# Gated DeltaNet on one Trainium2 core: gates moved behind the first taps, solver blocks transposed on 128 rows, weight subtractions shared out anew

## The chip, the cores and the metric

The kernel runs on one core of one Trainium2 chip. The core has five engines with an instruction queue each: PE (TensorE, matmuls into PSUM), ACT (ScalarE), DVE (VectorE), POOL (GpSimd) and SP (SyncE, which issues the DMAs here). Each queue runs in its written order; an instruction waits until what it reads has been written and what it overwrites has been read. The metric is the device time of one execution in microseconds (us). Before the change it was 2079.87 us, the median of three runs (2078.89 to 2080.14).

## The reference

The program is a decoder trunk of two layers over 512 tokens of width 1024. Each layer is a feed-forward block, a mixer, and another feed-forward block. The mixer of layer 0 is a convolution module; that of layer 1, which the change touches, is a chunked gated DeltaNet with 8 heads of 128 and chunks of 64 tokens. Cut to what matters:

```python
proj = h @ w_in                                  # q, k, v, z, and per head a, b
qkv = silu(causal_dwconv(qkv, w_sconv))          # 4 taps
g = -exp(a_log) * softplus(a + dt_bias)          # the gates
beta = sigmoid(b)
g = cumsum(g)                                    # within a chunk
decay = exp(where(causal, g_i - g_j, -inf))
A = where(strict, (k * beta) @ k.T * decay, 0)   # 64 x 64 for each head and chunk
Tm = inverse of (I + A), by a unit triangular solve
u = Tm @ (v * beta)
w = Tm @ (k * beta * exp(g))
# then a scan over the 8 chunks with a 128 x 128 state for each head
```

## The kernel before

All data lie with features (or tokens) on the 128 rows (partitions) of SBUF. Each weight block of 128 x 1024 is split into a rounded part and a rest, so that a product is three matmul passes: `hi` copies the loaded block `raw` to `whi` on ACT (L1071), `lo` subtracts to get `wlo` (L1077), and `mm3` (L172 to L174) does the passes. The list `LOP` says for which tiles `lo` runs on POOL; for the others it runs on DVE. Before, these are 4, 5 and 17 to 24.

**The steps.** The projection of the DeltaNet runs in a hand-written order. Tile 0 holds a and b, tiles 1 to 8 are the heads of k, 9 to 16 of q, 17 to 24 of v. Tiles 0 to 2 come from the stage before; `step(p)` computes tile p for p = 3 to 24 with 24 matmuls of 128 x 512, three for each k from 0 to 7. Between these matmuls it writes the work on earlier tiles into the engines' queues: after k = 0 `mul` (first tap, ACT, L1097) of tile p-1 and `hi` of p+2; after k = 1 the other taps of p-1 (`tap`, DVE, L1100), and on PE `tr` of p-2 (four transposes through PE, L1121), for which `silu` of p-2 (ACT, L1114, for q L1111) must be done; after k = 2 `fin` of p-2 and `lo` of p+2; after k = 5 `silu` of p-1. From tile 18 on, the third tap is a multiply on ACT (L1104) and an addition on POOL (`ptap`, L1105). `fin` takes the squares of k and q on ACT (L1044, L1132); for v it multiplies by beta into `vb`, in one DVE instruction (L1127).

**The gates.** `tok_in`, `small_gates` and `gates_math` make g and beta of all heads and tokens: three exponentials on ACT (L976 to L979) and some 20 operations of 128 x 32 on DVE (L971 to L1001). `first_evac`, in step 3, writes them among the taps of tiles 1 and 2. `cumulate` (L1006), `decay` (L1013) for each head, `decay_mask` and `decay_exp` follow; the tables `DEC`, `DXA` and `DXB` name step and k for each.

**The solver.** All 64 matrices I + A (8 heads, 8 chunks; two chunks lie above each other on the 128 rows) are inverted by their 32 x 32 diagonal blocks, as one batch on DVE. `blk_in` transposes the blocks from `am` into `blk`, one quarter (32 rows) at a time (four instructions, L1167). `solve_a` and `solve_b` (L1171, L1176), 31 of each, do a substitution; `blk_out` transposes the result into `rm` (four, L1181), `low_out` into `lm` (two, L1185). `merge_a` and `merge_b`, in steps 23 and 24, join the blocks. These tasks stand in a queue, each with a weight; `inv_run` takes tasks up to a weight at four places of each step from 13 on (`IQ`: 2, 2, 3 and 3). A transpose weighs `IW` = 3, a solver operation 1. `blk`, `tmp`, `tb` and `lm` are quarters of the buffer `x`, which is spilled to DRAM meanwhile.

Of the kernel before, what the change touches and what calls it, by code (L numbers as in the profile page):

```python
# [11 lines left out]
ALU = mybir.AluOpType  # L12
# [3 lines left out]
P = 128  # L16
# [44 lines left out]
EH = [1,2,3,3,5,6]  # L61
FH = [3,4,5,6]
EN = {(0,1):2,(0,2):3,(1,0):3,(1,1):3,(1,2):3}
LOP = [4,5,17,18,19,20,21,22,23,24]
IW = 3
IQ = [2,2,3,3]
DEC = [(5,4),(5,6),(6,4),(6,6),(7,4),(7,6),(8,4),(8,6)]
DXA = [(6,7),(8,7)]
DXB = [(7,7),(9,7)]
KBK = [(11,2),(11,4),(11,6),(12,0),(12,2),(12,4),(12,6),(13,0)]  # L70
ZF = 1
RQ = (22,6)
# [34 lines left out]
def trunk_kernel(ctx: ExitStack, tc: tile.TileContext, x_in, c_in, vecs, consts, w_ada, w_st,  # L107
# [827 lines left out]
    def deltanet(layer, nxt):  # L935
        NU = HEADS * NG
        norm = Norm()
        with tc.tile_pool(name=nm("dn"), bufs=1) as dp, \
# [27 lines left out]
            def tok_in():  # L966
                act.copy(tok.rearrange("p c h -> p (c h)"), st["pt"][:, :NG * 16])

            def small_gates():
                xa = sm()  # L970
                dve.tensor_tensor(xa, tok[:, :, :HEADS],  # L971
                                  V("dt_bias", 0, HEADS).unsqueeze(1).to_broadcast([P, NG, HEADS]), ALU.add)
                nx = sm()
                dve.scalar_tensor_tensor(nx, xa, -1.0, xa, ALU.mult, ALU.max)
                ea = scratch("ea", (P, HEADS))
                act.activation(ea, V("a_log", 0, HEADS), AF.Exp)  # L976
                act.activation(beta.rearrange("p h c -> p c h"), tok[:, :, HEADS:], AF.Exp, scale=-1.0)
                ey = sm()
                act.activation(ey, nx, AF.Exp, scale=-1.0)  # L979
                st["g"] = xa, ey, ea  # L980
# [87 lines left out]
            def hi(p):  # L1068
                whi = wp.tile([P, KT, P], F32R, tag="whi", name=nm("whi"))
                wlo = wp.tile([P, KT, P], F32R, tag="wlo", name=nm("wlo"))  # L1070
                act.copy(whi, raws[p])  # L1071
                W[p] = whi, wlo
# [22 lines left out]
            def mul(p):  # L1095
                ct[p] = scratch("t", bufs=2)
                act.mul(ct[p], ps[p], taps_w(p, 0))  # L1097
# [25 lines left out]
            def fin(p):  # L1123
                g, m = kind(p)
                pt = kx.pop(p)
                if g == "v":
                    dve.tensor_tensor(vb[:, :, m, :], pt.rearrange("p (c e) -> p c e", e=P),  # L1127
                                      beta[:, m, :].unsqueeze(2).to_broadcast([P, NG, P]), ALU.mult)
                    return
                squares(pt, m, ssk if g == "k" else ssq)  # L1130
                if g == "k":
                    act.copy(kt[:, :, m, :], pt.rearrange("p (c d) -> p c d", d=P))  # L1132
# [28 lines left out]
                pool.memset(rm[CH:, :, :], 0.0)  # L1161
                pool.memset(rm[:CH, :, :], 0.0)

            def blk_in(q):
                rows = slice(q * 32, (q + 1) * 32)
                c0 = (q % 2) * 32
                dve.transpose(blk[rows], am[rows, :, c0:c0 + 32].rearrange("p u j -> p j u"))  # L1167

            def solve_a(j):
                n = 31 - j  # L1170
# [3 lines left out]
            def solve_b(j):  # L1174
                n = 31 - j
                dve.tensor_tensor(tb[:, j + 1:, :j + 1], tb[:, j + 1:, :j + 1], tmp[:, :n, :j + 1], ALU.subtract)  # L1176

            def blk_out(q):
                rows = slice(q * 32, (q + 1) * 32)
                c0 = (q % 2) * 32  # L1180
                dve.transpose(box["rm"][rows, :, c0:c0 + 32].rearrange("p u i -> p i u"), tb[rows])  # L1181

            def low_out(q):
                rows = slice(q * 32, (q + 1) * 32)
                dve.transpose(lm[rows].rearrange("p u l -> p l u"), tb[rows].rearrange("p i l -> p l i"))  # L1185

            def inv_tasks():
                for q in range(4):
                    inv_q.append((IW, lambda q=q: blk_in(q)))
                for j in range(31):  # L1190
                    inv_q.append((1, lambda j=j: solve_a(j)))
                    inv_q.append((1, lambda j=j: solve_b(j)))
                for q in (3, 1, 2, 0):
                    inv_q.append((IW, lambda q=q: blk_out(q)))
                for q in (0, 2):
                    inv_q.append((IW, lambda q=q: low_out(q)))

            def inv_run(n):
                while n > 0 and inv_q:
# [116 lines left out]
            def on(p, k, f):  # L1316
                ex.setdefault(p, {}).setdefault(k, []).append(f)

            def first_evac():
                mul(1)  # L1320
                tok_in()
                small_gates()
                mul(2)
                for d in (1, 2, 3):
                    tap(1, d)
                gates_math()
                for d in (1, 2, 3):
                    tap(2, d)
                for p in (4, 5):
                    hi(p)  # L1330
                    lo(p)
                inv_fill()
                silu(1)
                silu(2)

            on(3, -1, tok_tr)
            on(3, 0, first_evac)
            on(4, 0, lambda: tr(1))
            on(4, 3, lambda: tr(2))
            on(4, 3, lambda: fin(1))  # L1340
            on(4, 4, lambda: fin(2))
            on(4, 4, cumulate)
            for h in range(HEADS):
                p, k = DEC[h]
                on(p, k, lambda h=h: decay(h))
# [422 lines left out]
```

## Time and profile before

| what | time |
|---|---|
| median of three runs | 2079.87 us |
| the profiled execution | 2082.37 us |
| its span, first to last instruction | 2080.6 us |
| the DeltaNet's steps 3 to 24 in it | 1345.63 to 1536.09 us |

A row of a view by groups gives line, engine, operation, what is written from what, shapes, count, then busy us and mean ns of one, then the idle time of the engine ahead of it and what ended it. A row in order of time gives start and duration in us. A row of a stretch gives its length, then for each engine the busy us and the number of instructions, then the granted PE clock and the DMA share.

### The profile page before, as it was taken

Reading aid. Unit: us, or ns where it says so; the run is one execution under the profiler, and the core shown is the slowest. Engines: PE = TensorE matmul, PEld = TensorE weight load, DVE = VectorE, ACT = ScalarE, POOL = GpSimd, SP = SyncE. Lnnn points to the kernel's source line nnn. Section 1 sums busy time; section 2 is a strip of 40 time slices with the busy share of each in tenths; the row PEclk is TensorE's granted clock in tenths of the full one; section 3 lists DMA queues with packets and bytes.
Section 4 is the critical chain, followed back from the end, with each engine's and each line's share of the span. In section 5 each row is a group of like instructions: output and inputs, shape, how many; then the busy total and the mean of one; then the engine's idle time right before and its main releaser. Section 6 shows DMA issues by size and latency. Waiting matters only on the chain.

```text
span 2080.6 us, 26152 instructions
## 1 busy us (share of the span) xinstructions
PE 2009.1 (97%) x10330; PEld 1677.3 (81%) x10330; DVE 1201.0 (58%) x1824; ACT 767.6 (37%) x1316; POOL 213.4 (10%) x145
## 2 busy tenths in 40 slices
PE   6999999998899999999999999989899999999998
PEld 4888888877898888888888888877677798888887
DVE  6666666798865656536333333677955564333334
ACT  5422222474642222224222222465356643222222
POOL 0000000299100000000000000125410100000000
PEclk9999999999899999999999999999899999999999
DMA  7667767322236666532333333322121132333331
GB/s 269 233 220 238 230 228 234 112 75 90 60 110 207 201 197 205 165 92 81 103 99 96 98 100 91 102 71 72 61 62 32 42 121 91 102 94 98 96 98 61
DMA packets 78333, 262.06 MB, mean 126 GB/s; under 512 B 8321, under 2 KB 14081, under 8 KB 78082
## 3 DMA queue, kind: packets, MB, share of 16 engines
q1 hardware_dynamic: 77666, 259.87, 39.2%
q8 instruction: 81, 1.33, 0.3%
q10 hardware_dynamic: 544, 0.52, 0.1%
q14 instruction: 42, 0.34, 0.0%
HBM read 254.59 MB, written 5.77 MB: 125 GB/s over the span
## 4 chain that ended last, share of the span: by engine, by line
PE 85%; DVE 7%; POOL 3%; ACT 2%; issue 2%; DMA 0%; POOLq 0%; DVEq 0%; SPq 0%; ACTq 0%
PE mm L172 26%; PE mm L173 26%; PE mm L174 26%; POOL pacc L671 3%; DVE t L1100 1%; PE mm L1425 1%; DVE x L1176 1%; DVE x L1171 1%; PE mm L1447 1%; PE mm L1652 1%; PE mm L1653 1%; PE mm L1433 1%; PE mm L1656 1%; PE mm L1415 1%; PE aux L639 1%
## 5 line engine op out<-in xcount | busy, mean ns | idle before, releaser
L172 PE MATMUL mm<-hh,whi 128*128 128x512 f32 (+1 forms) x1968 | 744.9, 380 | 5.4 <-ACT hh L273 3.7
L173 PE MATMUL mm<-hl,whi 128*128 128x512 f32 (+1 forms) x1968 | 738.5, 376 | 1.6 <-DVE hl L277 1.3
L174 PE MATMUL mm<-hh,wlo 128*128 128x512 f32 (+1 forms) x1968 | 736.7, 375 | 1.9 <-DVE wlo L164 1.9
L164 DVE TENSOR_TENSOR wlo<-raw,whi 128x1024 fp32r<-128x1024 f32 (+1 forms) x291 | 356.1, 1225 | 306.7 <-ACT whi L163 301.9
L172 PEld LDWEIGHTS mm<-hh,whi 128*128 128x128 f32 x1968 | 372.5, 190 | 74.2 <-ACT hh L273 4.5
L174 PEld LDWEIGHTS mm<-hh,wlo 128*128 128x128 f32 x1968 | 373.3, 190 | 69.7 <-DVE wlo L164 2.9
L173 PEld LDWEIGHTS mm<-hl,whi 128*128 128x128 f32 x1968 | 373.6, 190 | 68.3 <-DVE hl L277 3.7
L163 ACT CAST whi<-raw 128x1024 fp32r<-128x1024 f32 (+1 forms) x291 | 297.2, 1023 | 285.4 <-PE mm L173 258.2
L172 PE MATMUL mm<-ahi,whi 128*128 128x512 f32 (+1 forms) x768 | 289.3, 377 | 0.0
L174 PE MATMUL mm<-ahi,wlo 128*128 128x512 f32 (+1 forms) x768 | 287.0, 374 | 0.0
L173 PE MATMUL mm<-alo,whi 128*128 128x512 f32 (+1 forms) x768 | 284.7, 371 | 0.0
L540 ACT CAST ahi<-t 128x512 fp32r<-128x512 f32 x88 | 54.7, 622 | 371.0 <-DVE t L536 371.0
L174 PEld LDWEIGHTS mm<-ahi,wlo 128*128 128x128 f32 x768 | 144.6, 188 | 28.2
L173 PEld LDWEIGHTS mm<-alo,whi 128*128 128x128 f32 x768 | 144.8, 188 | 27.0
L172 PEld LDWEIGHTS mm<-ahi,whi 128*128 128x128 f32 x768 | 145.0, 189 | 24.2
L425 DVE CUSTOM_DVE_ANT_0 ajunk<-araw,cs 128x1024 bf16<-128x1024 f32 x128 | 156.1, 1219 | 0.6
L532 ACT ACTIVATE sil<-mm 128x512 f32<-128x512 f32 x88 | 52.6, 598 | 256.4 <-PE mm L174 256.4
L536 DVE TENSOR_TENSOR t<-sil,mm 128x512 f32<-128x512 f32 x88 | 60.4, 687 | 142.6 <-PE mm L174 141.0
L469 DVE SCALAR_TENSOR_TENSOR x<-mm,gate,x 128x512 f32<-128x512 f32 x64 | 48.1, 751 | 133.5 <-PE mm L174 133.5
L216 POOL TENSOR_TENSOR wlo<-raw,whi 128x1024 fp32r<-128x1024 f32 x6 | 14.4, 2397 | 837.8 <-ACT whi L215 837.8
L541 DVE TENSOR_TENSOR alo<-t,ahi 128x512 fp32r<-128x512 f32 x88 | 60.9, 692 | 60.5 <-ACT ahi L540 60.5
L671 POOL TENSOR_TENSOR pacc<-pacc,pr 128x492 f32<-128x492 f32 (+11 forms) x58 | 83.2, 1434 | 11.4 <-ACT pr L670 7.3
(261 smaller groups left out, 1709.4 us busy)
## 6 DMA issues: line engine op xcount, KB each, us to landing
raw<-in_w_fi_dram SPq DMA_DIRECT2D x169, 512.0 KB, 3.5
araw<-in_w_ada_dram SPq DMA_DIRECT2D x128, 512.0 KB, 4.6
raw<-in_w_fo_dram SPq DMA_DIRECT2D x64, 448.0 KB, 3.3
raw<-in_w_dn_dram SPq DMA_DIRECT2D x33, 512.0 KB, 3.6
raw<-in_w_fo_dram SPq DMA_DIRECT2D x32, 512.0 KB, 3.6
stage<-in_w_ada_dram SPq DMA_DIRECT2D x16, 512.0 KB, 6.5
raw<-in_w_glu_dram SPq DMA_DIRECT2D x16, 512.0 KB, 3.5
raw<-in_w_pw_dram SPq DMA_DIRECT2D x8, 512.0 KB, 3.6
```

The source lines that it names most:

```text
L163: act.copy(whi[:, :nk, :], raw[:, :nk, :])
L164: dve.tensor_tensor(wlo[:, :nk, :], raw[:, :nk, :], whi[:, :nk, :].bitcast(F32), ALU.subtract)
L172: pe.matmul(ps, whi[:, k, :], mhi, start=first, stop=False)
L173: pe.matmul(ps, whi[:, k, :], mlo, start=False, stop=False)
L174: pe.matmul(ps, wlo[:, k, :], mhi, start=False, stop=last)
L425: dve.tensor_tensor_reduce(junk, raw, ada["cs"], 1.0, 0.0, ALU.mult, ALU.add, accum_out=mod[:, layer, col:col + 1])
L469: dve.scalar_tensor_tensor(x[:, m, sl], ps, gate[:, j:j + 1], x[:, m, sl], ALU.mult, ALU.add)
L532: act.activation(s, g, AF.Silu)
L536: dve.tensor_tensor(pr, box["s"], u, ALU.mult)
L540: act.copy(ahi[:, jj, :], pr)
L541: dve.tensor_tensor(alo[:, jj, :], pr, ahi[:, jj, :].bitcast(F32), ALU.subtract)
L671: pool.tensor_tensor(pacc[m][:, c], pacc[m][:, c], pr[:, c], ALU.add)
```

## The change

Three things change, all in the DeltaNet's projection.

First, the order of steps 3 to 5. `first_evac` now has the multiply and taps of tiles 1 and 2 ahead, with `hi` of tile 4 in front, and the gates stand in a function of their own that step 4 calls after k = 3. `tr` and `fin` of tiles 1 and 2 and `cumulate` move by some places, the decays of heads 0 and 1 from step 5 to step 6, and the first mask and exponential by one step. Tiles 4 and 5 have their subtraction on DVE.

Second, the solver's transposes. Four ACT copies (`blk_copy`) gather the diagonal blocks into one tile, and one DVE transpose over all 128 rows takes them to `blk`. One DVE transpose takes the result to `tmp`, and four ACT copies (`blk_place`) put the blocks into `rm`. `low_out` becomes one transpose over 128 rows.

Third, `LOP` holds 18, 20, 22 and 24 only, and `vb` is made by four ACT multiplies instead of one DVE instruction.

```diff
-LOP = [4,5,17,18,19,20,21,22,23,24]
+LOP = [18,20,22,24]
-DEC = [(5,4),(5,6),(6,4),(6,6),(7,4),(7,6),(8,4),(8,6)]
-DXA = [(6,7),(8,7)]
-DXB = [(7,7),(9,7)]
+DEC = [(6,2),(6,4),(6,6),(7,2),(7,5),(8,2),(8,4),(8,6)]
+DXA = [(7,3),(8,7)]
+DXB = [(8,1),(9,7)]
...
                 if g == "v":
-                    dve.tensor_tensor(vb[:, :, m, :], pt.rearrange("p (c e) -> p c e", e=P),
-                                      beta[:, m, :].unsqueeze(2).to_broadcast([P, NG, P]), ALU.mult)
+                    for c in range(NG):
+                        act.mul(vb[:, c, m, :], pt[:, c * P:(c + 1) * P], beta[:, m, c:c + 1])
...
-            def blk_in(q):
+            tmq = x[:, 2:4, :].rearrange("p a (b c) -> p (a b) c", c=32)
+
+            def diag(t, q):
                 rows = slice(q * 32, (q + 1) * 32)
                 c0 = (q % 2) * 32
-                dve.transpose(blk[rows], am[rows, :, c0:c0 + 32].rearrange("p u j -> p j u"))
+                return t[rows, :, c0:c0 + 32]
+
+            def blk_copy(q):
+                act.copy(tmq[q * 32:(q + 1) * 32], diag(am, q))
+
+            def blk_in():
+                dve.transpose(blk, tmq.rearrange("p u j -> p j u"))
...
-            def blk_out(q):
-                rows = slice(q * 32, (q + 1) * 32)
-                c0 = (q % 2) * 32
-                dve.transpose(box["rm"][rows, :, c0:c0 + 32].rearrange("p u i -> p i u"), tb[rows])
-
-            def low_out(q):
-                rows = slice(q * 32, (q + 1) * 32)
-                dve.transpose(lm[rows].rearrange("p u l -> p l u"), tb[rows].rearrange("p i l -> p l i"))
+            def blk_out():
+                dve.transpose(tmp, tb)
+
+            def blk_place(q):
+                act.copy(diag(box["rm"], q).rearrange("p u i -> p i u"), tmp[q * 32:(q + 1) * 32])
+
+            def low_out():
+                dve.transpose(lm.rearrange("p u l -> p l u"), tb.rearrange("p i l -> p l i"))
 
             def inv_tasks():
                 for q in range(4):
-                    inv_q.append((IW, lambda q=q: blk_in(q)))
+                    inv_q.append((2, lambda q=q: blk_copy(q)))
+                inv_q.append((IW, blk_in))
                 for j in range(31):
                     inv_q.append((1, lambda j=j: solve_a(j)))
                     inv_q.append((1, lambda j=j: solve_b(j)))
+                inv_q.append((IW, blk_out))
                 for q in (3, 1, 2, 0):
-                    inv_q.append((IW, lambda q=q: blk_out(q)))
-                for q in (0, 2):
-                    inv_q.append((IW, lambda q=q: low_out(q)))
+                    inv_q.append((1, lambda q=q: blk_place(q)))
+                inv_q.append((IW, low_out))
...
             def first_evac():
+                hi(4)
                 mul(1)
-                tok_in()
-                small_gates()
                 mul(2)
+                lo(4)
                 for d in (1, 2, 3):
                     tap(1, d)
-                gates_math()
+                hi(5)
+                silu(1)
                 for d in (1, 2, 3):
                     tap(2, d)
-                for p in (4, 5):
-                    hi(p)
-                    lo(p)
+                tok_in()
+                silu(2)
+                lo(5)
                 inv_fill()
-                silu(1)
-                silu(2)
+
+            def first_gates():
+                small_gates()
+                gates_math()
 
             on(3, -1, tok_tr)
             on(3, 0, first_evac)
-            on(4, 0, lambda: tr(1))
-            on(4, 3, lambda: tr(2))
-            on(4, 3, lambda: fin(1))
-            on(4, 4, lambda: fin(2))
-            on(4, 4, cumulate)
+            on(4, 1, lambda: tr(1))
+            on(4, 2, lambda: fin(1))
+            on(4, 3, first_gates)
+            on(4, 4, lambda: tr(2))
+            on(4, 5, lambda: fin(2))
+            on(5, 3, cumulate)
```

What the change does to the engines' order is seen at two places. The first is ACT's queue in step 3, before. `ssum` is the copy of tile 0 (a and b) that the transposes at the head of step 3 read, `t` are the first taps of tiles 1 and 2, `whi` the casts of weights 4 and 5, `ea`, `beta` and `sm` the gates' exponentials.

```order
L1081 COPY ssum_10070<-mm_9834 16x512
L1097 ACTIVATE t_10094<-mm_9835,vec 128x512
L967 COPY tok<-aux_10086 128x64
L976 ACT_TABLE_LOAD
L976 ACTIVATE ea_10101<-vec 128x8
L977 ACTIVATE beta<-tok 128x4x8
L979 ACTIVATE sm_10104<-sm_10099 128x32
L1097 ACTIVATE t_10106<-mm_9836,vec 128x512
L1071 CAST whi_10137<-raw_10073 128x1024
L1071 CAST whi_10141<-raw_10075 128x1024
L1114 ACT_TABLE_LOAD
L1114 ACTIVATE sil_10147<-t_10094 128x512
```

The same place after the change:

```order
L1071 CAST whi_10094<-raw_10073 128x1024
L1081 COPY ssum_10070<-mm_9834 16x512
L1097 ACTIVATE t_10097<-mm_9835,vec 128x512
L1097 ACTIVATE t_10099<-mm_9836,vec 128x512
L1071 CAST whi_10105<-raw_10075 128x1024
L1114 ACT_TABLE_LOAD
L1114 ACTIVATE sil_10108<-t_10097 128x512
L967 COPY tok<-aux_10086 128x64
L1114 ACTIVATE sil_10114<-t_10099 128x512
```

The exponentials have moved behind both `silu`s, and the cast of weight 4 stands ahead of the copy of tile 0.

The second place is the end of the solver, in steps 20 to 22. DVE's queue before, from the last substitution on; `t` are the taps of tiles 20 and 21:

```order
L1176 TENSOR_TENSOR x<-x 128x31
L1181 STREAM_TRANSPOSE rm<-x 32x32x32 x2
L1100 SCALAR_TENSOR_TENSOR t_11356<-mm_11296,vec,t_11356 128x511
L1181 STREAM_TRANSPOSE rm<-x 32x32x32
L1100 SCALAR_TENSOR_TENSOR t_11356<-mm_11296,vec,t_11356 128x510
L1181 STREAM_TRANSPOSE rm<-x 32x32x32
L1127 TENSOR_TENSOR vb<-aux_11372,beta 128x4x128
L1185 STREAM_TRANSPOSE x<-x 32x32x32 x2
L1100 SCALAR_TENSOR_TENSOR t_11406<-mm_11352,vec,t_11406 128x511
```

DVE's queue after, at the same place:

```order
L1184 TENSOR_TENSOR x<-x 128x31
L1187 STREAM_TRANSPOSE x<-x 128x1024
L1100 SCALAR_TENSOR_TENSOR t_11363<-mm_11300,vec,t_11363 128x511
L1100 SCALAR_TENSOR_TENSOR t_11363<-mm_11300,vec,t_11363 128x510
L1193 STREAM_TRANSPOSE x<-x 128x32x32
L1077 TENSOR_TENSOR wlo_11369<-raw_11239,whi_11368 128x1024
L1100 SCALAR_TENSOR_TENSOR t_11417<-mm_11359,vec,t_11417 128x511
```

Six transposes have become two, and the subtraction of weight 23 stands behind the second. ACT's queue there after the change, from the multiply of tile 20 on (`sq` is the product of its third tap, `sil` of line 1114 its `silu`):

```order
L1097 ACTIVATE t_11363<-mm_11300,vec 128x512
L1104 ACTIVATE sq_11365<-mm_11300,vec 128x509
L1071 CAST whi_11368<-raw_11239 128x1024
L1190 COPY rm<-x 32x32x32 x4
L1128 ACTIVATE vb<-aux_11381,beta 128x128 x4
L1114 ACTIVATE sil_11403<-t_11363 128x512
L1097 ACTIVATE t_11417<-mm_11359,vec 128x512
```

The four copies into `rm` and the four products of `vb` now stand between the multiply of tile 20 and its `silu`; before, nothing stood there but the cast.

## Prediction

> **What bounds it now.** The page first: its span, and how much of it TensorE (PE) is busy.
>
> ```profile
> span 2080.6 us, 26152 instructions
> PE 2009.1 (97%) x10330; PEld 1677.3 (81%) x10330; DVE 1201.0 (58%) x1824; ACT 767.6 (37%) x1316; POOL 213.4 (10%) x145
> ```
>
> PE sets the time nearly everywhere, so an edit on other engines pays only where PE waits. Next, what PE waits for in the part that the change touches (the delta net's projection, 1345 to 1541 us):
>
> ```profile
> engine line waited for: us in total, times, longest us
> PE aux L1121 <- ACT sil L1114: 12.7, 7, 5.5
> PE aux L1121 <- ACT kq L1111: 6.1, 3, 2.8
> PE aux L1241 <- DVE cqn L1235: 1.2, 1, 1.2
> ```
>
> So 20 us, nearly all in `tr`: the transposes of tile p-2 stand early in step p, wait for ScalarE's (ACT's) `silu`, and that for VectorE's (DVE's) `tap`s. Which steps? Busy times by stretch, cut where a step's first matmul starts: step 4; 5; 14; 16 to 22 together; 18 alone; 23.
>
> ```profile
> core 0: us, PE busy (x) PEld busy (x) DVE busy (x) ACT busy (x) POOL busy (x), PEclk, DMA share, GB/s
> 1351.20:1366.18 14.98, 9.53 (x35) 7.25 (x34) 11.38 (x22) 6.62 (x24) 3.90 (x4) 0.77 0.30 81
> 1366.18:1373.94 7.76, 7.76 (x45) 6.70 (x44) 4.87 (x9) 3.78 (x12) 0.00 (x0) 1.00 0.35 115
> 1438.15:1444.08 5.93, 5.93 (x29) 4.89 (x28) 5.80 (x5) 2.77 (x10) 1.44 (x1) 1.00 0.05 18
> 1450.02:1510.57 60.55, 49.22 (x198) 38.41 (x196) 58.64 (x89) 20.43 (x49) 22.29 (x11) 0.89 0.22 65
> 1466.58:1476.43 9.85, 7.72 (x30) 5.99 (x28) 9.50 (x17) 3.19 (x11) 2.61 (x1) 0.83 0.24 76
> 1510.57:1521.08 10.51, 8.83 (x159) 6.88 (x157) 5.73 (x10) 7.13 (x11) 1.29 (x1) 1.00 0.15 50
> ```
>
> A step that nothing holds takes 5.93 us (24 matmuls, four transposes). Steps 16 to 22 take 60.55 where 7 x 5.93 = 41.5 would do: 19.0 held, and DVE is busy 58.64 of the 60.55, so DVE is their bound. Step 23 idles 10.51 - 8.83 = 1.7. A long wait costs twice: step 18 idles 9.85 - 7.72 = 2.1, yet is 3.9 over 5.93, since the granted clock falls to 0.83. That second 1.8 is to be added to a wait of over 2 us, unless DVE is late by more anyway.
>
> **Part one, the gates (steps 3 to 5).** Rows in order of time (start, duration) of DVE, GpSimd (POOL), PE and ACT around step 4, then groups (count | busy us, mean ns | idle before) of `silu` and its table load:
>
> ```profile
> 1349.35 2.39 DVE L990 TENSOR_TENSOR sm<-sm,sm 128x32 f32<-128x32 f32 x1
> 1351.78 2.32 DVE L992 TENSOR_TENSOR sm<-sm 128x32 f32<-128x32 f32 x1
> 1357.24 2.31 DVE L1100 SCALAR_TENSOR_TENSOR t<-mm,vec,t 128x511 f32<-128x511 f32 x3
> 1349.30 4.74 POOL L1077 TENSOR_TENSOR wlo<-raw,whi 128x1024 fp32r<-128x1024 f32 x2 [16.77 <-ACT whi L1071]
> 1360.33 1.11 PE L1121 MATMUL aux<-cst,sil 128*128 128x128 f32 x4 [5.45 <-ACT sil L1114]
> 1344.65 0.58 ACT L1081 COPY ssum<-mm 16x512 f32<-16x512 f32 x1 [2.97 <-PE mm L174]
> L1114 ACT ACT_TABLE_LOAD x3 | 3.8, 1283 | 2.0 <-DVE t L1100 2.0
> L1114 ACT ACTIVATE sil<-t 128x512 f32<-128x512 f32 x16 | 10.3, 645 | 40.1 <-DVE t L1100 40.1
> ```
>
> The taps of tile 2 start at 1357.24, behind the whole gate chain, which itself lost some 4 us where two tiny operations took 2.39 and 2.32 while POOL did its two subtractions. Hence the 5.45 wait. Unheld, step 4 would take 5.93 + 0.5 (a second `tr`) + 0.3 (`cumulate`) = 6.7: held 8.2, the slow clock included. The change puts both tiles' taps ahead of the gates and both subtractions on DVE, so both `silu`s end before step 4's transposes are due: **-8.2**. Two decays leave step 5 (7.76 - 5.93 = 1.8) for steps 6 to 8, which sums to nothing.
>
> What it adds: ACT's cast of weight 4 now stands ahead of the copy at 1344.65, on which step 3's first PE instruction depends. The cast takes 1.05 (below), and its buffer comes free only about one matmul (0.23, a 24th of a step's 5.5) before the copy may start, so **+0.8** (0 to 1.05). And ACT must pass the gates' exponentials and two table loads (2 x 1.28) in step 4 before `silu` of tile 3: 6.62 + 2.6 + 0.6 for that silu, less 1.3 for two silus that moved ahead and 1.5 for the squares that follow it, is 7.0 after the step's start, and PE asks at 6.7 + 1.4 = 8.1. I take nothing; without that cover, up to 2. Part one: **-7.4**, between -5 and -8.2.
>
> **Part two, the solver (steps 13 to 22).** DVE's groups from 1436 to 1511 us, and four single rows in order of time:
>
> ```profile
> L1176 DVE TENSOR_TENSOR x<-x 128x31 f32<-128x31 f32 (+15 forms) x31 | 18.8, 606 | 0.7
> L1171 DVE TENSOR_TENSOR x<-x 128x31 f32<-128x31 f32 (+15 forms) x31 | 16.9, 544 | 1.0
> L1100 DVE SCALAR_TENSOR_TENSOR t<-mm,vec,t 128x511 f32<-128x511 f32 (+2 forms) x22 | 16.4, 745 | 0.3
> L1167 DVE STREAM_TRANSPOSE x<-am 32x1024 f32<-32x1024 f32 x4 | 8.2, 2038 | 0.1
> L1181 DVE STREAM_TRANSPOSE rm<-x 32x1024 f32<-32x1024 f32 x4 | 8.0, 1994 | 0.1
> L1185 DVE STREAM_TRANSPOSE x<-x 32x1024 f32<-32x1024 f32 x2 | 4.3, 2142 | 0.0
> L1127 DVE TENSOR_TENSOR vb<-aux,beta 128x512 f32<-128x512 f32 x3 | 2.0, 679 | 0.0
> L1077 DVE TENSOR_TENSOR wlo<-raw,whi 128x1024 fp32r<-128x1024 f32 x1 | 1.2, 1226 | 0.0
> ...
> 1455.59 0.34 DVE L1176 TENSOR_TENSOR x<-x 128x175 f32<-128x175 f32 x1
> 1455.96 2.49 DVE L1171 TENSOR_TENSOR x<-x 128x192 f32<-128x192 f32 x1
> 1455.86 2.37 POOL L1077 TENSOR_TENSOR wlo<-raw,whi 128x1024 fp32r<-128x1024 f32 x1 [5.95 <-ACT whi L1071]
> 1480.11 1.36 DVE L1171 TENSOR_TENSOR x<-x 128x220 f32<-128x220 f32 x1
> ```
>
> These sum to 75.8 in 75 us: DVE is full. The single rows show a solver operation of about 0.35 that took 2.49 because POOL was subtracting, and one of about 0.4 that took 1.36 beside POOL's tap. So a subtraction on POOL costs DVE 2.1, and done by DVE itself 1.23. Off DVE: tiles 17, 19, 21 and 23 change over (4 x 0.9 = 3.5), seven of ten transposes go (14.3), vb goes (2.0): 19.8 in all. But PE gains only where DVE stays behind. DVE per step, after: taps 2.2 (from step 19 two: 1.5), solver 3.2, 4.1, 4.5, 4.4, 3.8, 2.6 (62 operations of 0.2 to 0.43, ten a step), a subtraction 1.23 or 2.1 in turn, about 1.0 behind POOL's tap in 19 and 20, a transpose in 20. That is 6.7, 8.4, 8.0, 8.7, 7.5 and 9.2 in steps 15 to 20, 48.5 against 6 x 5.93 = 35.6. About 1 us is in hand at step 15, so **11.9 stay held**, mostly before `tr` of steps 19 and 21. With step 23's 1.7, which goes because step 22 comes earlier, it was 20.7: **-8.8**.
>
> A transpose over 128 rows isn't in the trace. Its bounds are one of 32 rows (2.04) and four (8.15); I take 2.04, since prices here go with the columns, not the rows: ACT's copy of 16x512 took 0.58, its cast of 128x1024 (below) 1.05.
>
> **What the copies put back.** In step 21 ACT's queue holds four copies into `rm`, four vb products and only then `silu` of tile 20, for which PE waits in step 22; `mul` of 21 and its taps queue behind. ACT's rows for the price:
>
> ```profile
> L163 ACT CAST whi<-raw 128x1024 fp32r<-128x1024 f32 x227 | 236.9, 1045 | 173.6 <-PE mm L173 170.0 <-DMA raw<-in_w_pw_dram 2.1 <-DMA raw<-in_w_fi_dram 1.4
> L977 ACT ACTIVATE beta<-tok 128x32 f32<-128x32 f32 x1 | 0.2, 242 | 0.0
> L979 ACT ACTIVATE sm<-sm 128x32 f32<-128x32 f32 x1 | 0.2, 213 | 0.0
> L1445 ACT ACTIVATE t<-mm,cq 64x128 f32<-64x128 f32 x56 | 16.2, 357 | 1.3 <-PE mm L174 1.0
> ```
>
> From the end of the solver's one out-transpose, ACT needs 4p + 4 x 0.29 + 0.65, p being a copy. When does PE ask? Count from the last tap of tile 19: PE goes on 0.7 later (its `silu`), runs that `tr` (0.5), 18 matmuls of step 21 and six of step 22 (5.4), slow at first (1.8), and asks at 8.4; DVE ends the out-transpose at 3.3 (three solver operations, two more, 2.04). That leaves 5.1, and the hold is 4p - 3.3. A copy of 1024 elements in a row takes 1.05 (the cast). But these write single floats 256 bytes apart. The nearest rows for that are the two exponentials of 32 elements: L977 writes its floats 16 bytes apart and takes 29 ns more, 0.9 ns an element, so p = 1.05 + 0.93 = 2.0: a hold of 4.7, plus 1.8 for the clock, **+6.5**. The four copies in, in steps 13 and 14, write in rows and lie under free ACT time (2.77 of 5.93 busy); nothing.
>
> The Trainium skill, "SBUF — State Buffer", section "Door 1: The DMA port swizzle", speaks against these copies: accesses that go to a new 16-byte line each time pay a penalty. It names no size; going by it the copies lie above 1.05, which is the case that I take from L977, whereas DVE's transposes into the same places (L1181, 1.99) are no slower than L1167 (2.04), which writes in rows. The skill's "TensorE: Matmul & The Clock Gate", section "HAM oscillation — how this bites in real kernels", wants gaps of over 3.4 us before the clock falls; the row at 1466.58 has 0.83 after 2.1, so the measurement decides. By the page, step 18 would not have paid its 1.8.
>
> **Sum.** -7.4 - 8.8 + 6.5 = -9.7 from the profiled execution's 2082.37. The median of the runs is 2.5 lower, 2079.87; so 2070.2.
>
> **Rivals.** (a) The copies run at the cast's rate: 4 x 1.05 - 3.3 = 0.9 and no slow clock, -15.3 in all: **2064.6**. For it: L1181 beside L1167. (b) The gates, pushed into step 4, make a new wait: `silu` of tile 3 or `cumulate` in step 5 comes late by 2 and brings the clock's 1.8, so the sum is -5.9: **2074**. Against it: a margin of 1.1 us in ACT's queue. (c) A transpose over 128 rows takes four turns, 8.15: the one in puts 6.1 more into step 14 and the first out 6.1 into step 20, both held; the second out lies in step 21 beside the copies: 12.2 above the forecast, **2082.4**, no change that can be told. (d) The other side: a scattered copy costs ACT several times a plain one. The sum is -7.4 - 8.8 - 3.3 + 1.8 + 4p = -17.7 + 4p, over zero from p = 4.4; at p = 6 it is +6.3: **2086.2**. Against it: 0.9 ns an element in L977. That the moves don't take place is excluded by the order of instructions.
>
> **Numbers.** Forecast 0.5 (own range 2067 to 2073), (a) 0.28, (b) 0.12, (c) 0.06, (d) 0.04. The range 2062 to 2075 takes in the first three; its low end adds to (a) the bound of part one, -8.2, and a little. A measurement of this kernel can tell about 0.2% (4.2 us) from no change: faster 0.89, same 0.07, slower 0.04.
>
> **What would show it.** Right: no PE wait in step 4; the copy L1081 about 0.8 later; waits before `tr` in steps 19, 21 and 22, none in 16 or 23; a 128-row transpose near 2 us; copies into `rm` near 2 us. Wrong: copies near 1.05 (then a); a wait in step 5 (b); transposes over 4 us (c); PE waiting in step 22 for over 8 us (d).

## The result and the profile after

The changed kernel takes **2065.56 us** (median of 4 runs, 2064.65 to 2066.42) where the kernel before takes 2079.38 (median of 4, 2078.20 to 2080.14): a ratio of 0.9933, with a 95% interval from 0.9921 to 0.9946, or 13.8 us less. The forecast was 2070.2 with a range of 2062 to 2075: the right side and inside the range, but the gain was forecast 4 us too small (9.7 against 13.8). The profiled execution of the changed kernel took 2064.65.

The page of the changed kernel, its span and the busy time of each engine:

```profile
span 2062.8 us, 26172 instructions
PE 1997.0 (97%) x10330; PEld 1669.5 (81%) x10330; DVE 1174.2 (57%) x1815; ACT 789.1 (38%) x1357; POOL 198.2 (10%) x139
```

DVE has lost 26.8 us and ACT has gained 21.5, and still the span only fell by 17.8. Shares can't say more than that; the waits of PE can. Its waits between 1335 and 1545 us in the changed kernel (us in total, times, longest):

```profile
PE aux L1121 <- ACT sil L1114: 10.2, 3, 5.4
PE aux L1121 <- ACT kq L1111: 2.2, 2, 1.2
PE aux L1056 <- issue: 1.4, 1, 1.4
PE aux L964 <- ACT ssum L1081: 0.8, 1, 0.8
```

The wait before `tr` in step 4 is gone, as is the one for `cqn` in step 23. A new wait of 5.4 us is the longest now, and the copy L1081 has brought its 0.8.

To see where the time went, both traces are cut at the same events: at the end of the last `hh` activation ahead of the projection, and at the end of the four transposes of tiles 3, 13, 19, 22 and 24 (tile t's `tr` stands in step t+2). Five rows for before, then five for after (stretch, its length, busy time and count of each engine, granted clock, DMA share, GB/s):

```profile
1341.68:1368.16 26.48, 21.03 (x104) 17.32 (x103) 17.96 (x34) 14.75 (x36) 5.79 (x4) 0.87 0.20 60
1368.16:1446.05 77.89, 76.70 (x505) 62.93 (x505) 55.09 (x76) 51.23 (x139) 34.26 (x24) 1.00 0.21 62
1446.05:1495.77 49.72, 41.50 (x169) 32.45 (x169) 47.93 (x82) 17.84 (x53) 18.28 (x8) 0.90 0.24 74
1495.77:1523.18 27.41, 22.62 (x217) 17.67 (x217) 20.35 (x20) 13.27 (x21) 8.56 (x5) 0.94 0.20 58
1523.18:1539.85 16.67, 15.74 (x294) 12.21 (x295) 9.84 (x16) 8.46 (x13) 2.56 (x2) 1.00 0.32 98
```

```profile
1338.18:1356.91 18.73, 17.95 (x102) 15.34 (x101) 13.51 (x29) 14.20 (x36) 0.00 (x0) 1.00 0.30 85
1356.91:1434.99 78.08, 76.90 (x507) 63.16 (x507) 50.57 (x84) 57.72 (x146) 34.45 (x24) 1.00 0.20 62
1434.99:1478.82 43.83, 37.98 (x169) 30.34 (x169) 42.18 (x79) 19.88 (x60) 9.91 (x5) 0.96 0.28 84
1478.82:1506.87 28.05, 22.68 (x216) 18.33 (x217) 10.54 (x13) 24.22 (x37) 6.18 (x4) 0.88 0.19 58
1506.87:1523.92 17.05, 15.63 (x294) 12.38 (x295) 9.14 (x15) 10.51 (x21) 2.99 (x3) 1.00 0.34 94
```

Row by row: -7.8 up to tile 3 (the gates), +0.2 up to tile 13, -5.9 up to tile 19 (the solver), +0.6 up to tile 22 (the copies into `rm`), +0.4 behind, where PE's wait at L1056 has grown to 1.4 for a reason that the profile doesn't name; **-12.4** in all. In the fourth row DVE's 20.35 fall to 10.54 and ACT's 13.27 rise to 24.22 of 28.05: the bound has moved from DVE to ACT there. The changed stretch accounts for 12.4 of the 13.8 between the medians; the rest is taken up by the last experiment.

Steps 19 to 23 of the changed kernel apart, from one tile's `tr` to the next:

```profile
1454.28:1464.28 10.00, 6.49 (x29) 5.17 (x29) 9.65 (x16) 3.54 (x13) 2.39 (x1) 0.96 0.34 107
1464.28:1471.42 7.14, 7.14 (x29) 5.81 (x29) 6.90 (x14) 4.45 (x10) 1.74 (x2) 0.82 0.00 0
1471.42:1478.82 7.40, 6.13 (x30) 4.83 (x29) 7.09 (x14) 2.83 (x8) 3.38 (x2) 1.00 0.50 142
1478.82:1490.78 11.96, 6.59 (x29) 5.28 (x29) 5.68 (x5) 11.90 (x14) 1.29 (x1) 0.86 0.15 44
1490.78:1498.33 7.55, 7.55 (x29) 6.08 (x29) 2.23 (x5) 5.92 (x11) 3.99 (x3) 0.78 0.23 69
```

An unheld one takes 5.93. Up to the third row DVE is busy nearly throughout; in the fourth, which ends with the 5.4 us wait for tile 20's `silu`, DVE is busy 5.68 and ACT 11.90 of 11.96. The second and the fifth row have no wait at all and are long only by the clock, 0.82 and 0.78, after a long wait in the row ahead.

The new operations in the changed kernel, by groups (count | busy us, mean ns | idle before):

```profile
L1190 ACT COPY rm<-x 32x1024 f32<-32x1024 f32 x4 | 7.9, 1983 | 0.1
L1172 ACT COPY x<-am 32x1024 f32<-32x1024 f32 x4 | 4.2, 1046 | 0.8 <-DVE am L1057 0.7
L1193 DVE STREAM_TRANSPOSE x<-x 128x1024 f32<-128x1024 f32 x1 | 2.2, 2217 | 0.0
L1175 DVE STREAM_TRANSPOSE x<-x 128x1024 f32<-128x1024 f32 x1 | 2.1, 2104 | 0.7 <-ACT x L1172 0.7
L1187 DVE STREAM_TRANSPOSE x<-x 128x1024 f32<-128x1024 f32 x1 | 1.2, 1246 | 0.0
```

Two rows of its gate chain on DVE, in order of time (start, duration):

```profile
1354.67 0.19 DVE L990 TENSOR_TENSOR sm<-sm,sm 128x32 f32<-128x32 f32 x1
1354.89 0.19 DVE L992 TENSOR_TENSOR sm<-sm 128x32 f32<-128x32 f32 x1
```

A transpose of 128 rows costs what one of 32 did, or less; the copies into `rm` cost 1.98, those in 1.05; and the two tiny gate operations that took 2.39 and 2.32 beside POOL's subtractions take 0.19 now that POOL is idle.

### The profile page after: what moved, and what is told of

It is laid out like the page before. It is cut to its first block, busy times and chain, and to the rows that moved or that the text cites. A ratio compares the mean times of both kernels' runs of the same rounds, so it can differ in the third digit from the quotient of the medians.

```text
span 2062.8 us, 26172 instructions
## 1 busy us (share of the span) xinstructions
PE 1997.0 (97%) x10330; PEld 1669.5 (81%) x10330; DVE 1174.2 (57%) x1815; ACT 789.1 (38%) x1357; POOL 198.2 (10%) x139
## 4 chain that ended last, share of the span: by engine, by line
PE 87%; DVE 5%; POOL 3%; ACT 3%; issue 2%; DMA 0%; POOLq 0%; DVEq 0%; SPq 0%; ACTq 0%
PE mm L172 26%; PE mm L173 26%; PE mm L174 26%; POOL pacc L671 3%; PE mm L1438 1%; DVE x L1179 1%; PE mm L1460 1%; PE mm L1665 1%; PE mm L1666 1%; PE mm L1446 1%; PE mm L1669 1%; PE mm L1428 1%; DVE x L1184 1%; DVE t L1100 1%; PE aux L376 1%
```

## Experiments

The stretch from the anchor to tile 24 repeats to a few tenths from kernel to kernel wherever nothing in it was edited, while medians of whole runs scatter by one to three microseconds. So each experiment is read in its stretch. All durations below are from the traces, cut as above; the median stands with that of the kernel before in the same set of runs. The durations are taken in nanoseconds, so they can differ by 0.01 from the rows.

| kernel | median (before) | to tile 3 | 3 to 13 | 13 to 19 | 19 to 22 | 22 to 24 | sum |
|---|---|---|---|---|---|---|---|
| before | 2079.38 | 26.48 | 77.89 | 49.73 | 27.41 | 16.67 | 198.2 |
| after | 2065.56 (2079.38) | 18.72 | 78.08 | 43.83 | 28.05 | 17.06 | 185.7 |
| gates_only | 2071.14 (2080.16) | 18.72 | 78.08 | 49.74 | 27.42 | 16.67 | 190.6 |
| no_gates | 2071.55 (2080.16) | 26.27 | 77.92 | 43.85 | 28.01 | 16.67 | 192.7 |
| rows_place | 2061.90 (2080.16) | 18.72 | 78.08 | 43.84 | 22.60 | 16.67 | 179.9 |
| places_late | 2069.55 (2080.16) | 18.73 | 78.08 | 43.83 | 30.64 | 16.74 | 188.0 |
| places_dve | 2061.46 (2079.66) | 18.72 | 78.09 | 43.82 | 25.09 | 16.68 | 182.4 |
| sub_dve | 2060.90 (2079.66) | 18.73 | 78.08 | 39.68 | 28.88 | 16.78 | 182.1 |
| sub_pool | 2066.82 (2079.66) | 18.72 | 78.09 | 46.89 | 28.40 | 16.70 | 188.8 |
| vb_dve | 2063.56 (2079.66) | 18.72 | 78.08 | 44.55 | 27.47 | 16.67 | 185.5 |
| blocks_only | 2067.56 (2078.65) | 18.72 | 78.09 | 47.35 | 27.71 | 16.68 | 188.5 |
| out_twice | 2066.16 (2078.65) | 18.73 | 78.08 | 43.83 | 28.88 | 17.33 | 186.9 |
| all_three | 2054.31 (2078.65) | 18.92 | 78.20 | 39.67 | 20.55 | 16.69 | 174.0 |
| before_again | 2079.17 (2079.00) | 26.13 | 77.93 | 49.74 | 27.45 | 16.68 | 197.9 |

### One part alone

**gates_only**: the kernel before with the new `first_evac`, `first_gates` and decays.

```diff
-LOP = [4,5,17,18,19,20,21,22,23,24]
+LOP = [17,18,19,20,21,22,23,24]
-DEC = [(5,4),(5,6),(6,4),(6,6),(7,4),(7,6),(8,4),(8,6)]
+DEC = [(6,2),(6,4),(6,6),(7,2),(7,5),(8,2),(8,4),(8,6)]
...
+            on(4, 3, first_gates)
```

> The kernel before with part one alone (first_evac, first_gates, their hooks, the decays' places, subtractions 4 and 5 on DVE). Theory one, the forecast's: step 4 is tied to nothing behind it, so part one is worth 7.4 us by itself: 2072.0 against 2079.4, no wait for sil L1114 in step 4, a wait of 0.8 before L964, waits of steps 16 to 23 as before. Theory two: the trace of after is 11.3 us ahead at tile 3's tr (1356.91 against 1368.16), and all of it is part one: 2068. If part one leans on the other parts (its silus need ACT free), under 4 us.

**no_gates**: the changed kernel with `first_evac`, the gates' places, the decays and the subtractions of tiles 4 and 5 as before (`LOP = [4,5,18,20,22,24]`).

> The changed kernel with part one undone: 128-row transposes, vb on ACT, subtractions of v in turn. Theory one: the parts add up, so -13.8 + 7.4 = -6.4: 2073, and it was part two that was forecast too small (-2.3). Theory two: part one was worth 11, and part two only what was forecast: 2076.5 to 2077. Waits in steps 17 to 22 as in after: 1.0, 0.1, 3.5, 1.3, 5.4 before tr.

By the trace the gates alone are worth 26.48 - 18.72 = 7.8, less 0.2 up to tile 13, and everything behind stays as it was (49.74 against 49.73). Without them the first column is back (26.27) and the rest is as in after. So the two parts hardly touch each other: 7.6 and 5.5 (198.2 - 192.7) make 13.1, and both together 12.4; 0.4 of the difference is the last column (17.06 in after, 16.67 in both of these). Which of part one's edits does it, the order of the queues or the two subtractions taken off POOL, these runs don't separate. Theory two (11 us) fell: some 3.5 of that lead lies ahead of the anchor, where both kernels have the same instructions. The medians, 9.0 and 8.6 less than before, would have put the sum of the parts at 17.6 and suggested that the parts stand in each other's way by nearly 4 us, which the stretches don't show.

### The copies into rm

**rows_place** writes 32 floats in a row. It leaves out the swap of the two indices, so it computes something else; it only prices the write:

```diff
-                act.copy(diag(box["rm"], q).rearrange("p u i -> p i u"), tmp[q * 32:(q + 1) * 32])
+                act.copy(diag(box["rm"], q), tmp[q * 32:(q + 1) * 32].rearrange("p a b -> p (a b)").rearrange("p (a b) -> p a b", b=32))
```

> The changed kernel, its four copies into rm writing 32 floats in a row instead of single floats 256 bytes apart; this leaves out the swap of the two indices in these copies. Theory one: the scattered write is what makes them 1.98 us; in rows they take 1.05, the hold in step 22 falls by 4 x 0.93 = 3.7 to 1.7 and its slow clock goes (1.8): 5.5 less than after, 2060. Theory two: it is the read of 32 rows behind DVE's transpose, or ACT itself, and not the write: 1.9 or more and no gain. Theory three: the copies do fall to 1.05, but tile 20's taps are late next (DVE, POOL), and the gain is under 2 us.

The same group in this kernel's trace:

```profile
L1190 ACT COPY rm<-x 32x1024 f32<-32x1024 f32 x4 | 4.2, 1048 | 0.1
```

1.98 became 1.05, the wait in step 22 fell from 5.37 to 1.74, and tiles 19 to 22 take 22.60 instead of 28.05: 5.45 less. Of that 3.6 is the shorter wait (the four copies are 4 x 0.93 = 3.7 shorter), and the other 1.8 goes with the slow clock, which is at 1.00 there now. Theory one held in every term. The scattered write is the price, and nothing else is late next.

**places_late** moves the copies behind the `silu`s.

```diff
-                for q in (3, 1, 2, 0):
-                    inv_q.append((1, lambda q=q: blk_place(q)))
-                inv_q.append((IW, low_out))
...
+BOUT = [(21,5),(21,5),(22,5),(22,5)]
+            for (p, k), q in zip(BOUT, (3, 1, 2, 0)):
+                on(p, k, lambda q=q: blk_place(q))
+            on(22, 2, low_out)
```

> The changed kernel with the four copies into rm moved in ACT's queue: two behind silu of tile 20 (end of step 21), two behind silu of tile 21 (end of step 22); nothing else moves but low_out, which goes to step 22. Theory one: only their place ahead of silu of tile 20 costs PE, so the wait of 5.4 and the slow clock's 1.8 in step 22 go, and about 3 come back since ACT now does mul and silu of tiles 21 and 22 late (8.1 us of ACT work in a step of 5.9): 4 less than after, 2061.5. Theory two: 7.9 us of ACT work must go somewhere, and the same 7 us only move to steps 23 and 24: 2065. Theory three: nothing behind is late: 2058.

It got slower than after, 30.64 instead of 28.05. The row of PE in this kernel with its longest wait (idle before it, and what ended that):

```profile
1498.60 0.69 PE L1248 MATMUL aux<-cqn,cst 128*128 128x64 f32 x2 [5.29 <-DVE cqn L1242]
```

And ACT's rows ahead of it:

```profile
1491.93 4.17 ACT L1191 COPY rm<-x 32x1024 f32<-32x1024 f32 x2
1496.11 1.28 ACT L1048 ACT_TABLE_LOAD   x1
1497.40 0.32 ACT L1048 ACTIVATE ssq<-ssq,eps 128x32 f32<-128x32 f32 x1
```

Step 22's wait did go, but the second pair of copies now stood ahead of ACT's square root for `rq_fin`, on which DVE's `cqn` and then PE's `rq_swap` in step 23 depend. The wait is named after DVE, but what it waits for is ACT: DVE had been idle for 4.4 us before its reciprocal, waiting for `ssq`. No theory had it slower than after. Theory two had the mechanism: the time only moved, to step 23; but it came back larger: over the 20.4 that these three take unheld (5.93 + 5.93 + 8.54) it is 10.2 us, where after has 7.65.

**places_dve** takes the work off ACT: no out-transpose of 128 rows; DVE transposes each quarter straight into `rm`, behind the taps.

```diff
-            def blk_out():
-                dve.transpose(tmp, tb)
-
-            def blk_place(q):
-                act.copy(diag(box["rm"], q).rearrange("p u i -> p i u"), tmp[q * 32:(q + 1) * 32])
+            def blk_out(q):
+                dve.transpose(diag(box["rm"], q).rearrange("p u i -> p i u"), tb[q * 32:(q + 1) * 32])
...
+BOUT = [(21,2),(21,5),(22,2),(22,5)]
...
+            on(23, 2, low_out)
```

> The changed kernel without the out-transpose of 128 rows and without the four copies into rm: DVE transposes the four quarters straight into rm (2.0 each), two behind the subtraction and the silu of step 21, two in step 22, low_out in step 23. Theory one: what holds step 22 is only that ACT does 7.9 us of copies ahead of silu of tile 20; DVE has 5.93 - 2.8 = 3.1 free in each of steps 21 to 23, so the wait of 5.4 and 2.3 of slow clock go: tiles 19 to 22 take 20.4 instead of 28.05, 2058. Theory two, from places_late: whatever engine takes the 8 us, rq_fin's chain or tile 21's taps come late by it in steps 23 and 24, and the same 7 us stay: 2065. Between them, if two transposes of 2.0 beside 2.8 of taps and subtraction hold step 22's taps: 1 to 2 lost.

25.09: 3.0 of the 7.65 that after is held there. Step 22 runs unheld, but the last two quarters stand on DVE ahead of `rq_fin`'s reciprocal, and PE waits for `cqn` in step 23 and then pays the slow clock:

```profile
1494.14 0.69 PE L1244 MATMUL aux<-cqn,cst 128*128 128x64 f32 x2 [2.95 <-DVE cqn L1238]
```

It is the same place as in places_late, by another engine, and theory two's mechanism at a smaller price: it costs 25.1 - 20.4 = 4.7, between theory one's nothing and theory two's 7. One of this kernel's five runs took 2072.80, the others 2061.14 to 2064.01; why is not known.

### The subtractions and vb

**sub_dve** (`LOP = []`), **sub_pool** (`LOP = [17,18,19,20,21,22,23,24]`), and **vb_dve**, which has before's line for `vb`:

```diff
-                    for c in range(NG):
-                        act.mul(vb[:, c, m, :], pt[:, c * P:(c + 1) * P], beta[:, m, c:c + 1])
+                    dve.tensor_tensor(vb[:, :, m, :], pt.rearrange("p (c e) -> p c e", e=P),
+                                      beta[:, m, :].unsqueeze(2).to_broadcast([P, NG, P]), ALU.mult)
```

> The changed kernel with all weight subtractions on DVE. Theory one, the forecast's prices: a subtraction on POOL stops DVE for 2.1, on DVE it takes 1.23; numbers 18, 20 and 22 lie where DVE is the bound, so tiles 13 to 19 take 43.83 - 3 x 0.87 = 41.2. Theory two: the long solver operations beside POOL have another cause, and POOL takes 1.23 each off DVE: 43.83 + 3.7 = 47.5. The total moves by the same, but is read by the stage, since runs of one kernel lie 2 us apart.

> The changed kernel with subtractions 17 to 24 all on POOL, as before the change. Theory one: 17, 19 and 21 cost 0.87 more each in DVE-bound steps, tiles 13 to 19 take 46.4; the alternation was worth 2.6 of the 5.3 of part two. Theory two (no stop): 40.1. Theory three: DVE has 1 us in hand at step 15 and hides some, 45.

> The changed kernel with vb on DVE again. Theory one: vb of tiles 17 and 18 (0.68 each) stands ahead of taps in DVE-bound steps 19 and 20, tiles 13 to 19 take 1.4 more (45.2); in step 22 four products (1.15) leave ACT's queue ahead of silu of tile 20, 1.1 less plus a little clock (tiles 19 to 22 26.7): in all nothing, 0.0 to 0.3. Theory two: DVE still has gaps and only ACT's queue counts: 1.3 faster. Theory three: ACT's queue isn't what holds step 22 but DVE: 1.4 slower or more.

Tiles 13 to 19 take 39.68 with all subtractions on DVE, 43.83 with every second on POOL, 46.89 with all on POOL. Each that goes from DVE to POOL costs, as theory one had it: three cost 3.06 (2.6 expected). Three the other way gave 4.15. With them the wait of 3.5 us before tile 17's `tr` shrinks to 1.3, and the granted clock of this stretch is 1.00 instead of 0.96:

```profile
1459.83 0.66 PE L1121 MATMUL aux<-cst,sil 128*128 128x128 f32 x4 [1.30 <-ACT sil L1114]
```

That a spell of slow clock makes the 1.5 above 3 x 0.87 is argued, not shown. Behind tile 19, sub_dve gives 0.8 back, since PE comes earlier to a step 22 that the copies still hold, and the last column takes 0.3 less; 3.6 less than after are left for the whole stretch. So the alternation is only about half of what is to be had here. Moving `vb` to ACT gained nothing: 0.72 less between tiles 13 and 19, 0.58 and 0.39 more behind. That was nearest to theory one, which had the two nearly cancel.

**blocks_only** puts both together: subtractions 17 to 24 all on POOL and `vb` on DVE, so only the transposes and copies are left of part two.

> The changed kernel with the subtractions of tiles 17 to 24 all on POOL and vb on DVE, so that of part two only the transposes and copies are left. Theory one: the parts add up: 13 to 19 46.89 + 0.72 = 47.6, 19 to 22 28.40 - 0.58 = 27.8, together 75.4 against 77.1 before and 71.9 after: the transposes and copies by themselves are worth 1.7, and the alternation most of part two's gain. Theory two: they lean on each other (DVE late enough hides a part), 73 to 74 or over 76.5.

47.35 + 27.71 = 75.1, against 77.1 in before: the transposes with their copies are worth 2.1 us (190.6 - 188.5 for the whole stretch), and the alternation with `vb` 2.8 (188.5 - 185.7). Theory one, to 0.4.

### The out-transpose twice

```diff
             def blk_out():
                 dve.transpose(tmp, tb)
+                dve.transpose(tmp, tb)
```

> The changed kernel with the solver's out-transpose done twice, one directly behind the other. Theory one: it stands behind tile 19's last tap, so it can hold nothing up to tr of tile 19: tiles 13 to 19 stay at 43.83, and only the copies start 0.8 to 1.25 later: 19 to 22 28.9 to 29.3, the wait in step 22 6.2 to 6.6. The forecast's 11.9 counted that transpose (and five solver operations behind the tap) into steps 15 to 20, which would be wrong by 2 to 3. Theory two, the forecast's own count: tiles 13 to 19 take 1.25 more.

The two stretches of this kernel:

```profile
1436.49:1480.32 43.83, 38.01 (x169) 30.24 (x169) 42.18 (x79) 19.88 (x60) 9.89 (x5) 0.96 0.27 84
1480.32:1509.20 28.88, 22.64 (x216) 18.36 (x217) 11.67 (x14) 24.20 (x37) 6.20 (x4) 0.88 0.19 56
```

DVE's rows around the cut, in order of time:

```profile
1478.14 0.74 DVE L1100 SCALAR_TENSOR_TENSOR t<-mm,vec,t 128x510 f32<-128x510 f32 x1
...
1480.04 1.25 DVE L1187 STREAM_TRANSPOSE x<-x 128x1024 f32<-128x1024 f32 x1
1481.32 1.25 DVE L1188 STREAM_TRANSPOSE x<-x 128x1024 f32<-128x1024 f32 x1
```

The first stretch is the same to the hundredth, the second 0.83 longer. The row at 1478.14 is tile 19's last tap: the transposes come behind it, so nothing up to tile 19's `tr` can wait for them. The copies behind them, and so step 22, can.

### A version that beats both

**all_three**: `LOP = []`; the quarters on DVE as in places_dve, but spread so that none stands ahead of `cqn` in step 22; and the cast of weight 4 behind `mul(1)`, to take back the 0.8 before L964.

```diff
-LOP = [18,20,22,24]
+LOP = []
+BOUT = [(21,2),(22,7),(23,3)]
...
+                inv_q.append((IW, lambda: blk_out(3)))
...
+            on(23, 5, low_out)
...
-                hi(4)
                 mul(1)
+                hi(4)
```

> The changed kernel with three edits: all weight subtractions on DVE; DVE transposes the quarters straight into rm, one ahead of tile 20's taps, one behind them in step 21, one behind rq_fin's reciprocal in step 22, one in step 23 (low_out behind it); the cast of weight 4 behind mul of tile 1, so behind the copy L1081. Theory one: the waits are apart and each goes: anchor to tile 3 17.9 (the 0.8 before L964), tiles 13 to 19 39.7 as in sub_dve, 19 to 22 20.4 (no wait in step 22, cqn of step 23 no later than PE asks), 22 to 24 16.7: 13 less than after, 2052. Theory two: DVE, now with 8 us of transposes and all subtractions, is late for cqn or tile 22's taps in step 23 by 2 to 3, with the clock 4: 2056. Theory three: the cast of weight 4 only changes place with tap 1 of tile 1, and step 4's tr of tile 2 waits instead: 17.9 becomes 18.7 or more.

Its stretches:

```profile
1339.02:1357.94 18.92, 18.09 (x102) 15.26 (x101) 13.22 (x28) 13.65 (x33) 0.00 (x0) 1.00 0.26 84
1357.94:1436.14 78.20, 77.01 (x507) 63.09 (x507) 50.82 (x86) 58.11 (x149) 34.46 (x24) 1.00 0.20 61
1436.14:1475.82 39.68, 36.39 (x170) 29.08 (x169) 38.20 (x79) 19.90 (x60) 2.89 (x2) 1.00 0.26 80
1475.82:1496.37 20.55, 20.55 (x216) 16.69 (x217) 18.82 (x20) 15.99 (x32) 3.88 (x3) 1.00 0.35 104
1496.37:1513.06 16.69, 15.80 (x294) 12.31 (x295) 9.57 (x16) 10.91 (x21) 2.62 (x3) 1.00 0.30 96
```

2054.31 us, a ratio of 0.9880 to before with an interval of 0.9863 to 0.9896: below that of after (0.9921 to 0.9946). Between tiles 19 and 22 PE is busy all 20.55 us and the clock is at 1.00 in every row. Two of the three edits did what theory one said; the third did nothing: 18.92 instead of 17.9. The 0.8 before L964 is gone, and in its place stands a wait before tile 3's `tr` in step 5:

```profile
1357.28 0.66 PE L1122 MATMUL aux<-cst,sil 128*128 128x128 f32 x4 [0.83 <-ACT sil L1115]
```

PE gets there 0.7 earlier, and with the cast behind `mul(1)` ACT's `silu` of tile 3 starts 17.6 behind the anchor instead of 17.0. Theory three had 18.7 or more, but at tile 2's `tr` in step 4.

### What the stretch doesn't explain

> The kernel before, profiled once more, unchanged. In the stretch that the change touches (last hh activation ahead of the projection to tr of tile 24) after takes 185.7 us where the first profile of before takes 198.2: 12.4 less, while the medians lie 13.8 apart, and in the other kernels of this study the medians show 0 to 3.4 more than the stretch does. Theory one: what lies ahead of it differs from execution to execution (1336.5 to 1339.7 in eleven kernels with the same instructions there, 1341.7 in the first profile of before): this profile shows 1336 to 1340 ahead, and 198.2 in the stretch again. Theory two: the kernel before is slower ahead of the change or behind it for a reason of its own: 1341 to 1342 again, and 540.7 behind. The stretch within 0.3 of 198.2 under both.

The kernel before once more took 1339.99 us to the anchor, 197.9 in the stretch and 540.74 from tile 24 to the end. Its stretch repeats to 0.3. Ahead of the anchor the kernels lie between 1336.5 and 1341.7, with the same instructions: theory one there. Behind tile 24 both profiles of before have 540.7, after and four others 538.8 to 538.9, the rest 538.0 to 540.9, with the same instructions but for `vb` of tile 24, which doesn't sort them (538.0 to 540.9 with it on ACT, 539.2 to 540.7 on DVE). What sets these microseconds wasn't tried, and stays open. The 1.4 by which the medians differ more than the stretch is within them.

## Why the prediction was right, and where it was off

**Part one, -7.4: right.** Measured -7.6, alone and in company. The 0.8 for the cast came as a wait of 0.78 before L964; the steps up to tile 13, into which the decays moved, take 0.2 more (forecast nothing); no wait in steps 4 and 5. Rival (b), a new wait in step 5, stayed away, but by less than the margin of 1.1 that the forecast gave ACT. The rows of tile 3 in the changed kernel, ACT's and PE's:

```profile
1355.22 0.63 ACT L1114 ACTIVATE sil<-t 128x512 f32<-128x512 f32 x1
```

```profile
1356.31 0.60 PE L1121 MATMUL aux<-cst,sil 128*128 128x128 f32 x4
```

`silu` ends at 1355.85, 0.46 ahead of `tr`; in all_three that was used up.

**Part two, the steps 15 to 20, "11.9 stay held": this is the step that failed.** Tiles 13 to 19 took 43.83, which is 8.25 over 6 x 5.93. The forecast had added up DVE's work step by step and put the out-transpose (2.04) into step 20; and it had then let the same transpose, and the solver operations behind tile 19's last tap, open the account of step 22 ("DVE ends the out-transpose at 3.3"). These 3.3 were counted twice. out_twice shows it for the transpose: doubling it moved this stretch by nothing. The five solver operations stand behind the same tap in DVE's queue, but weren't tested. Without them the forecast's own figures give 11.9 - 3.3 = 8.6, and 8.25 was measured. The waits sit where it said (3.5 in step 19, 1.3 in step 21), with a small one in step 17 (1.0).

**The price of the transposes: 2.04 taken, right for two of three.** 2.10 and 2.22; but 1.25 for the out-transpose, both sides of which lie in rows. The trace of before had none of that kind, so 2.04 was no lower bound. Rival (c), 8.15, fell.

**The copies: p = 2.0 taken from L977, measured 1.98**, and 1.05 with the scatter taken away, as rival (a) had it for its own case: the difference between the forecast and (a) was 5.6, and rows_place measured 5.45. So the price of a scattered element, read from two operations of 32 elements that differ by 29 ns, came out right; two single rows were a thin ground for it, and that they hit it so closely may be luck. The time fell close to (a)'s 2064.6 by another cause, so the number alone would have confirmed the wrong rival. Rival (d) fell with p.

**Step 22, +6.5: mechanism right, size 1.1 too small.** Wait 5.37 instead of 4.7, with 2.3 of slow clock around it (11.96 + 7.55 - 2 x 5.93 = 7.65). The forecast let PE ask late because step 21 would run at a slow clock; but step 21's wait was 1.26 and the clock stayed at 1.00. PE asked 6.9 after tile 19's last tap instead of 8.4, and the copies began 2.8 after it instead of 3.3.

**Together**: -0.2 in part one, -3.6 in steps 16 to 21, +1.1 in step 22, and within 0.4 behind it (which cancel: 0.4 more was held in before than the forecast's 20.7, and 0.4 came in the last row) make the 2.7 between the forecast's -9.7 and the stretch's -12.4. The last 1.4 up to the medians' 13.8 is the scatter told above.

## What to carry to other kernels

Where work is counted step by step on an engine, cut at the instruction that another engine waits for, not at the end of the step: what stands behind that instruction holds nothing yet, and belongs to the next account. Work moved to an idle engine is only free if nothing urgent is queued behind it there: here 7.9 us on an ACT that was 38% busy cost 7.65, and the same work on DVE, spread between its deadlines, left 0.15 there (all_three). Measure an edit of some microseconds in its own stretch, cut at the same events in both traces: that repeats to 0.1 to 0.3 us where whole runs differ by 2.

## What the runs showed of the hardware that was not expected

**Where the clock falls.** The forecast added 1.8 us to each wait of over 2 us of PE. That served here, but the length of the wait isn't what decides. Between 1340 and 1545 us of these traces the granted clock is 1.00 or 0.50; a spell of 0.50 lasts 3.41 us or a whole multiple of it and begins on a grid of that step. What counts is how long PE idles within one window of the grid. In before, the wait of 2.13 and the window that holds it, with the next:

```profile
1470.23 0.66 PE L1121 MATMUL aux<-cst,kq 128*128 128x128 f32 x4 [2.13 <-ACT kq L1111]
```

```profile
1467.85:1471.26 3.41, 1.28 (x9) 0.94 (x8) 3.24 (x8) 1.71 (x3) 0.00 (x0) 1.00 0.29 112
1471.26:1474.67 3.41, 3.41 (x10) 2.66 (x9) 3.33 (x3) 1.47 (x9) 2.61 (x1) 0.50 0.02 5
```

PE idles 2.13 of the 3.41, and the clock is 0.50 for the whole of the next window. The longest wait behind which it stayed at 1.00 is 1.98, in vb_dve, and it lies across the edge of two windows, of which the second and the one behind it are:

```profile
1477.23 0.66 PE L1121 MATMUL aux<-cst,sil 128*128 128x128 f32 x4 [1.98 <-ACT sil L1114]
```

```profile
1475.93:1479.35 3.42, 2.12 (x12) 1.83 (x13) 3.27 (x8) 2.72 (x4) 0.88 (x1) 1.00 0.12 47
1479.35:1482.76 3.41, 3.41 (x17) 2.83 (x16) 2.93 (x3) 3.38 (x2) 0.41 (x1) 1.00 0.01 2
```

Only 1.30 of it falls into this one. So 1.98 and 2.13 don't bracket a limit. What does are rows_place, first, with all of a wait of 1.74 in one window, and gates_only with 1.95 of a wait of 2.31:

```profile
1484.91:1488.33 3.42, 1.68 (x10) 1.13 (x10) 1.63 (x2) 3.42 (x9) 0.03 (x1) 1.00 0.20 72
1488.33:1491.74 3.41, 3.41 (x17) 2.81 (x16) 1.50 (x2) 2.28 (x6) 3.41 (x2) 1.00 0.21 82
```

```profile
1474.22:1477.63 3.41, 1.46 (x9) 1.29 (x10) 3.24 (x9) 2.14 (x4) 0.28 (x1) 1.00 0.34 132
1477.63:1481.05 3.42, 3.42 (x10) 2.66 (x9) 3.38 (x2) 0.58 (x1) 3.42 (x2) 0.50 0.00 0
```

In this stretch of all fourteen traces a window at full clock that idled up to 1.74 was followed by 1.00, and one that idled 1.95 or more by 0.50. So the same wait can cost the clock or not, by where it falls. It is no limit for all work: near 525 us, in another stage of after, a window that idled 1.19 was followed by 0.50. A spell of 3.41 us at 0.50 costs a busy PE half of it, 1.7, near the forecast's 1.8. The Trainium skill, "TensorE: Matmul & The Clock Gate", section "HAM oscillation — how this bites in real kernels", wants idle gaps of over 3.4 us before the clock falls, and ties the figure to a window. The gap isn't borne out here, where 2.13 was enough; the window is, by the spells of 3.41.

**A transpose pays for its strides, not for its rows.** A transpose took 1.25 us for 128x1024 with both sides in rows (L1187), 2.10 and 2.22 with one side or both strided (L1175, L1193), and 2.04 for 32x1024 with one side strided. ACT pays about as much for a scattered write (1.98 against 1.05, where strides cost DVE's transposes 0.86 to 0.97). This agrees with the penalty that the Trainium skill names in "SBUF — State Buffer", section "Door 1: The DMA port swizzle", and the size here is 0.91 ns an element.
